# A decoder layer on one core: another task order in the front, other engines for copies, other PSUM banks

## The chip, the cores and the metric

The kernel runs on one core of a Trainium2 chip. The core has five engines, each with its own queue of instructions that it works off in order: PE (TensorE, matrix products; PEld is its weight load), DVE (VectorE), ACT (ScalarE), POOL (GpSimd) and SP (SyncE, which here issues the DMAs). The metric is the device time of one execution in microseconds (us). The kernel before takes 786.61 us, the median of 3 runs (784.54 to 787.06).

## The reference

One layer for 512 positions of width 1024, in float32: an input projection feeds two mixers side by side, an attention with 8 query heads and 2 key/value heads (compressed blocks, selected blocks and a sliding window, each with its own keys and values, mixed by gates), and a diagonal state-space model (S5) with 32 groups of 16 channels and 64 complex states each. Both are normalised, joined and projected; then comes a feed-forward part with a causal convolution of width 3. Cut to what matters:

```
mod = silu(c) @ w_ada + b_ada;  sh1, sc1, gt1, sh2, sc2, gt2 = split(mod, 6)
h = rmsnorm(x, norm1_g) * (1 + sc1) + sh1
zq, zkc, zvc, zks, zvs, zkw, zvw, zg, zs = split(h @ w_in)
o_attn = nsa_attention(zq, zkc, zvc, zks, zvs, zkw, zvw, sigmoid(zg), pe_k, pe_v, w_ck1, w_ck2, w_cv1, w_cv2)
y_ssm = s5_mixer(zs, lam_re, lam_im, log_step, b_re, b_im, c_re, c_im, d_skip, w_glu, b_glu)
x = x + gt1 * (concat(rmsnorm(o_attn), rmsnorm(y_ssm)) @ w_o)
h = rmsnorm(x, norm2_g) * (1 + sc2) + sh2
a, v = split(causal_dwconv(h @ w_up, conv_w, conv_b))
x = x + gt2 * ((silu(a) * v) @ w_down);  return rmsnorm(x, normf_g)
```

In the S5 mixer the state is x(t) = a x(t-1) + B u(t), complex, scanned over the positions; the output is Re(C x) + D u, then GELU and a gated projection (GLU).

## The kernel before

Activations and weights of the large products are split into a high part, rounded to float32r, and a low part, the rest; each product is three float32r matmuls (mm3, L120 to L123: high by high, high by low, low by high). A weight block is loaded by one DMA into a raw buffer, and split into a unit buffer (weights, L111; split, L107): the high half is a cast, whose engine is the entry h_NAME, the low half a subtraction, whose engine is e_NAME. Buffers are few: 4 raw ones, 4 units, 3 small "sw" tiles, and 8 PSUM banks in four groups (acc 3, tr 2, ms 2, pv 1).

The front is written as about 200 small tasks (L143 to L1138), which the string ORDER (L19) calls one after the other (L1140):

- ident to z7: x is normalised and transposed (xn), the modulation columns are computed from w_ada (a and p for the first norm, b and s for the second, g1 for the gate), and z0 to z7 scale one slice of 128 channels each, split it and multiply it for the S5 input (zs, four PSUM banks).
- W, U, L: the block operators of S5 (W0 to W3; We is the copy of a transposed block out of PSUM) and its inputs (U) give the block states X (L).
- zk, zv, kx: keys and values; rope turns q and k (L605), ko is the rotated key, kx transposes it (KS, E), VT holds the values and GT the gates.
- chain (L694): the scan over X. Seven steps l1 to l7 run one after the other, then six short ones (c1 to c6), then eight steps a0 to a7 that add the carried state. Each step is madd (L685): a product (L689), a sum (L691) and an addition to X (L692), on the engine e_l1 to e_a7.
- AM0, AM1 (L727), hid, comp: the compressed blocks plus their position rows, their product with w_ck1 and w_cv1 from raw buffers, a GELU (cg) and a second small product.
- zq, qx: the queries. zq0 to zq3 sum into banks of group acc, of which there are three; rope then reads the bank.
- VV (L957), XV (L964), K, Y: S5's output operators. VV0 to VV7 are two products and a sum each (L348, L349); the second product goes to an "sw" tile (vw). XV copies X in four parts to zu: XV00, XV01, XV10, XV11, each 64 partitions by 1024. K makes the block kernel M through kz and DMAs; Y is the product, yT its transpose, ge the GELU (high and low half yh), gl the GLU (mx is its scaled copy).
- S, O (L807, L872): scores, softmax and output of one query block (qt) and two heads; sm is the scaling of the exponentials, pT the transposed probabilities and pz the compressed ones, copied out of PSUM.
- R, F, N (L1100, L908, L924): the output projection of the S5 half and of the attention half with the addition to x (os, oa), and the second norm (h2).
- eu, eup, cv: the first two up-weight blocks and their products over 384 positions.

After the tasks come two loops over 22 blocks of the feed-forward width: up (L1160; g is the product of the two halves, gc the copy of the gate row) and down (L1203; gh is g split in high and low), and the tail that normalises and stores the output.

Choices stand in the dictionary PICK (L18). kn(name, options) (L30) returns the entry of PICK, or the first option if there is none. e_NAME is the engine of a copy or an elementwise operation (V DVE, A ACT, P POOL), h_NAME the engine of a high half, ps_NAME the group of PSUM banks, r_NAME the kind of buffer.

The order of instructions on each engine is settled when the program is built: the tile layer (schedule_with_timeline_sim, L1304) takes the instructions in the order in which the tasks issue them as priorities, and lets a later one pass where an earlier one is not ready by its own timeline. So instructions of several tasks stand mixed in one queue; on the chip each queue is then strictly in order.

Of the kernel before, what the change touches and what calls it, by code (L numbers as in the profile page):

```python
# [14 lines left out]

PICK = {'ps_mg10': 'pv', 'ps_mg11': 'pv', 'ps_mg13': 'pv', 'ps_mb0': 'pv', 'ps_mb1': 'pv', 'ps_mb2': 'pv', 'ps_mb3': 'pv', 'ps_mc0': 'pv', 'ps_mc1': 'pv', 'ps_mc2': 'pv', 'ps_mc3': 'pv', 'e_bt11a': 'V', 'e_U001': 'A', 'e_U110': 'V', 'e_U111': 'A', 'e_U200': 'V', 'e_U301': 'A', 'e_U310': 'V', 'ps_sc030': 'ms', 'ps_p3101': 'ms', 'e_We5': 'V', 'e_Z0': 'V', 'e_mx1': 'P', 'e_sm10100': 'A', 'ps_hid01': 'tr', 'e_W3': 'V', 'ps_up6': 'ms', 'e_yh1': 'P', 'xn1': 'pt', 'e_inv2': 'P', 'e_g0': 'P', 'ps_p3111': 'ms', 'e_sm00011': 'P', 'e_mx2': 'V', 'e_mx0': 'P', 'e_h21': 'V', 'ps_up7': 'tr', 'e_tl300': 'V', 'e_GT0': 'P', 'e_sm30001': 'V', 'e_ro63': 'P', 'e_ro80': 'P', 'e_ro82': 'P', 'e_ro83': 'P', 'e_XV11': 'V', 'e_Y6': 'V', 'ps_oa3': 'acc', 'e_gh7': 'P', 'e_gh3': 'P', 'e_gh5': 'P', 'e_tl311': 'V', 'e_gt21': 'V', 'e_sm20101': 'P', 'ps_h23': 'tr', 'e_kt1': 'V', 'e_sm21001': 'P', 'ps_p0100': 'ms', 'e_os0': 'V', 'ps_W5': 'tr', 'ps_kx3': 'ms', 'e_GT3': 'P', 'ps_mrp0': 'pv', 'e_tl001': 'V', 'e_tl011': 'V', 'e_tl100': 'V', 'e_tl101': 'V', 'e_tl111': 'V', 'e_tl200': 'V', 'e_inv1': 'P', 'e_inq1': 'P', 'e_inq0': 'P', 'e_inq2': 'P', 'e_inq3': 'P', 'ps_hid10': 'tr', 'e_glu0': 'V', 'e_os3': 'V', 'e_dg0': 'P', 'e_h23': 'V', 'ps_mra1': 'pv', 'ps_eup1': 'pv', 'e_sm21000': 'V', 'e_sm10101': 'V', 'e_XV01': 'P', 'e_Y7': 'V', 'ps_gt21': 'acc', 'e_sm00110': 'V', 'e_kt6': 'V', 'ps_cv': 'ms', 'how_g20': 'VP', 'e_hid01': 'V', 'e_hid11': 'V', 'e_sm30010': 'V', 'tl001': 'sw', 'tl101': 'sw', 'e_sm00111': 'V', 'ps_kx1': 'ms', 'e_E30': 'V', 'e_kt7': 'V', 'ps_ssqa3': 'pv', 'ps_h21': 'tr', 'ps_hid11': 'tr', 'e_kt5': 'V', 'e_dn5': 'P', 'e_h20': 'V', 'ps_h22': 'acc', 'h_ps1010': 'P', 'h_ps2111': 'P', 'h_ink0': 'V', 'h_dn0': 'V', 'e_sm11111': 'P', 'h_h21': 'V', 'h_up20': 'P', 'h_up01': 'V', 'h_up11': 'P', 'h_up30': 'V', 'h_up40': 'V', 'h_up41': 'V', 'h_inq3': 'V', 'e_sm21111': 'P', 'ps_xT2': 'ms', 'ps_xT0': 'ms', 'ps_xT1': 'ms', 'ps_xT3': 'ms', 'e_Z1': 'A', 'e_os20': 'V', 'hx3': 'pt', 'e_E20': 'V', 'e_oT101': 'P', 'h_oa1': 'V', 'h_oa3': 'V', 'ps_pc200': 'pv', 'mixa3': 'pt', 'h_dn2': 'V', 'ps_p2112': 'ms', 'h_gh1': 'V', 'e_dn2': 'P', 'e_os11': 'V', 'h_h20': 'P', 'h_yh2': 'V', 'ps_gt20': 'tr', 'e_Wc0': 'V', 'e_sy2': 'V', 'e_Z3': 'A', 'h_gh0': 'V', 'h_gh4': 'V', 'hx2': 'pt', 'h_dn3': 'P', 'e_g1': 'P', 'e_sm20111': 'P', 'e_sm00000': 'A', 'e_sm00101': 'P', 'e_sm01001': 'P', 'e_sm01011': 'P', 'e_sm01100': 'V', 'e_sm01101': 'P', 'e_sm01110': 'A', 'e_sm10000': 'A', 'e_sm10011': 'P', 'e_sm11000': 'V', 'e_sm11101': 'P', 'e_sm20001': 'P', 'e_sm20011': 'P', 'e_sm21011': 'P', 'e_sm30111': 'P', 'e_sm31111': 'P', 'ps_U0': 'tr', 'e_Y2': 'V', 'e_th101': 'V', 'h_inq0': 'V', 'e_xn0': 'P', 'ps_L2': 'tr', 'e_pt2111': 'P', 'ps_p3102': 'ms', 'e_oT011': 'P', 'e_a7': 'P', 'e_pt1010': 'P', 'e_kt3': 'V', 'e_pt0010': 'P', 'e_kt2': 'V', 'e_inv3': 'P', 'h_yh3': 'V', 'e_XV00': 'P', 'r_adab00': 'mid', 'r_adac00': 'mid', 'r_adac10': 'mid', 'r_adac11': 'mid', 'r_adac21': 'pt', 'r_adac30': 'mid', 'r_adac31': 'mid', 'r_adag100': 'pt', 'r_adag101': 'mid', 'ada_g20': 'V', 'r_adag110': 'mid', 'r_adag111': 'mid', 'ada_g21': 'V', 'r_adag120': 'mid', 'r_adag121': 'mid', 'ada_g22': 'V', 'r_adag130': 'mid', 'r_adag131': 'mid', 'ada_g23': 'V', 'e_up181': 'P', 'r_adab11': 'pt', 'e_l4': 'V', 'h_up180': 'P', 'e_ro60': 'P', 'e_ro81': 'P', 'e_gh2': 'P', 'h_gh15': 'V', 'e_gl2': 'V', 'e_Wc3': 'A', 'e_up111': 'P', 'e_oa2': 'V', 'h_up121': 'V', 'e_Wc1': 'A', 'ps_zv0': 'tr', 'e_up51': 'P', 'e_gh20': 'P', 'h_up140': 'P', 'e_Y1': 'V', 'e_os01': 'V', 'e_U101': 'A', 'e_gh11': 'P', 'ada_c2': 'V', 'ps_pc001': 'ms', 'e_hid00': 'V', 'e_gc3': 'V', 'e_up141': 'P', 'e_Wc7': 'A', 'ps_W2': 'tr', 'h_dn12': 'P', 'e_dn20': 'P', 'e_xn2': 'P', 'h_up141': 'P', 'h_gh8': 'V', 'e_sm31100': 'V', 'h_dn6': 'P', 'h_up81': 'P', 'e_tl310': 'V', 'e_dn10': 'P', 'ps_up9': 'ms', 'e_up190': 'P', 'h_gh10': 'V', 'h_up21': 'V', 'h_up130': 'V', 'h_inv3': 'V', 'h_up101': 'P', 'e_pT2012': 'V', 'h_gh5': 'V', 'e_pz101': 'V', 'e_dn12': 'P', 'e_g8': 'P', 'ps_up4': 'tr', 'e_up21': 'P', 'e_pT3101': 'A', 'ps_up13': 'tr', 'e_up90': 'P', 'h_inv0': 'P', 'e_up50': 'P', 'ps_up8': 'tr', 'e_VV6': 'P', 'e_up60': 'P', 'e_We00': 'V', 'e_up161': 'P', 'h_dn17': 'V', 'ps_up18': 'ms', 'e_sm00001': 'P', 'e_rowa1': 'V', 'js': '0', 'ps_mg20': 'pv', 'e_x2': 'V', 'e_sm10111': 'P', 'e_sm01010': 'V', 'e_W11': 'V', 'e_pz211': 'V', 'h_dn15': 'V', 'e_g13': 'P', 'e_pT3001': 'A', 'e_pT3003': 'A', 'e_sm30110': 'V', 'e_sm20010': 'V', 'e_L11': 'V', 'e_oT3': 'V', 'e_g15': 'P', 'e_os31': 'V', 'e_dg6': 'P', 'e_E10': 'V', 'h_ins0': 'V', 'e_up160': 'P', 'pz100': 'sw', 'ps_L3': 'tr', 'ps_q3': 'ms', 'e_kz2': 'V', 'e_g12': 'P', 'h_up51': 'P', 'h_up190': 'V', 'ps_p1010': 'acc', 'e_We30': 'V', 'e_A4': 'V', 'ps_up19': 'ms', 'ps_pc000': 'ms', 'e_pz300': 'V', 'e_glu1': 'V', 'e_gh4': 'P', 'e_We01': 'V', 'h_inq1': 'V', 'ps_co0': 'ms', 'h_up90': 'V', 'e_We10': 'V', 'e_gt11': 'V', 'e_ko1': 'V', 'e_U211': 'A', 'e_g5': 'P', 'e_up80': 'P', 'e_gl3': 'V', 'e_xn1': 'A', 'e_pT3100': 'V', 'e_a4': 'V', 'h_up31': 'P', 'e_W21': 'V', 'e_mh33': 'V', 'h_gh11': 'V', 'h_up80': 'V', 'e_sm31011': 'P', 'e_up200': 'P', 'e_U010': 'V', 'h_dn1': 'P', 'h_up70': 'V', 'h_ins1': 'P', 'e_kz4': 'V'}  # L18
# [1289 lines left out]
```

## Time and profile before

| | |
|---|---|
| median of 3 runs | 786.61 us |
| profiled execution | 788.21 us, span 786.4 us |
| PE busy | 725.1 us (92%) |
| DVE busy | 473.5 us (60%) |
| ACT busy | 290.2 us (37%) |
| POOL busy | 298.1 us (38%) |
| mean granted clock of PE | 0.957 |
| DMA | 87.64 MB, mean 111 GB/s |

The span is the time from the first to the last instruction. A busy time is the sum of an engine's instructions. PE's ends are modelled, so a busy PE need not run at its peak; the granted clock is a share of full speed. In a timeline row the columns are start and duration in us, engine, line of the kernel, operation, what is written and read, the shape and the count; in brackets stands how long the engine stood idle before it and whose instruction ended that.

### The profile page before, as it was taken

Reading aid. Unit: us, or ns where it says so; the run is one execution under the profiler, and the core shown is the slowest. Engines: PE = TensorE matmul, PEld = TensorE weight load, DVE = VectorE, ACT = ScalarE, POOL = GpSimd, SP = SyncE. Lnnn points to the kernel's source line nnn. Section 1 sums busy time; section 2 is a strip of 40 time slices with the busy share of each in tenths; the row PEclk is TensorE's granted clock in tenths of the full one; section 3 lists DMA queues with packets and bytes.
Section 4 is the critical chain, followed back from the end, with each engine's and each line's share of the span. In section 5 each row is a group of like instructions: output and inputs, shape, how many; then the busy total and the mean of one; then the engine's idle time right before and its main releaser. Section 6 shows DMA issues by size and latency. Waiting matters only on the chain.

```text
span 786.4 us, 11211 instructions
## 1 busy us (share of the span) xinstructions
PE 725.1 (92%) x4155; PEld 566.2 (72%) x4155; DVE 473.5 (60%) x1034; ACT 290.2 (37%) x603; POOL 298.1 (38%) x286
## 2 busy tenths in 40 slices
PE   3897999867899999989979999999999999999993
PEld 2576787555567666757769888888888888888883
DVE  2459938279666878585575576666554454333337
ACT  7443334111576755355423232332242322212123
POOL 2687548887121425254551142120333103130023
PEclk9799999988989999979979999999999999999997
DMA  8665245751121034000053133334232324223102
GB/s 266 234 247 194 95 156 170 288 185 57 29 52 33 1 147 175 2 0 5 1 188 134 54 113 129 138 131 133 108 131 83 108 81 134 108 81 107 54 1 107
DMA packets 30843, 87.64 MB, mean 111 GB/s; under 512 B 4712, under 2 KB 9252, under 8 KB 30757
## 3 DMA queue, kind: packets, MB, share of 16 engines
q1 hardware_dynamic: 30789, 86.92, 32.3%
q8 instruction: 33, 0.54, 0.3%
q14 instruction: 21, 0.17, 0.1%
HBM read 82.71 MB, written 2.10 MB: 108 GB/s over the span
## 4 chain that ended last, share of the span: by engine, by line
PE 75%; DVE 10%; POOL 7%; ACT 3%; DMA 2%; issue 2%; SPq 0%; POOLq 0%; ACTq 0%; DVEq 0%
PE up L123 9%; PE up L121 9%; PE up L122 9%; PE dn L123 5%; PE dn L121 5%; PE dn L122 5%; PE sc L827 3%; PE p L892 2%; PE po L898 2%; DVE vw L348 1%; PE eup L121 1%; PE eup L123 1%; PE eup L122 1%; PE y L1012 1%; POOL prl L689 1%
## 5 line engine op out<-in xcount | busy, mean ns | idle before, releaser
L123 PE MATMUL up<-h2h,uup 128*128 128x512 f32 x320 | 126.4, 395 | 0.0
L121 PE MATMUL up<-h2h,uup 128*128 128x512 f32 x320 | 126.3, 396 | 0.0
L122 PE MATMUL up<-h2l,uup 128*128 128x512 f32 x320 | 126.0, 394 | 0.0
L1175 DVE SCALAR_TENSOR_TENSOR us<-up,cst,us 128x511 f32<-128x511 f32 x80 | 59.8, 747 | 64.4 <-ACT us L1173 63.2
L1173 ACT ACTIVATE us<-up,cst 128x512 f32<-128x512 f32 x40 | 31.1, 778 | 107.9 <-PE up L123 107.9
L123 PEld LDWEIGHTS up<-h2h,uup 128*128 128x128 f32 x320 | 60.1, 188 | 14.1
L122 PEld LDWEIGHTS up<-h2l,uup 128*128 128x128 f32 x320 | 60.0, 188 | 14.2
L121 PEld LDWEIGHTS up<-h2h,uup 128*128 128x128 f32 x320 | 60.1, 188 | 14.0
L123 PE MATMUL dn<-udn,ghs 128*128 128x512 f32 x176 | 68.5, 389 | 0.0
L122 PE MATMUL dn<-udn,ghs 128*128 128x512 f32 x176 | 68.5, 389 | 0.0
L121 PE MATMUL dn<-udn,ghs 128*128 128x512 f32 x176 | 68.0, 389 | 0.0
L109 POOL TENSOR_TENSOR uup<-rup,uup 128x1024 fp32r<-128x1024 f32 x13 | 33.0, 2540 | 49.8 <-ACT uup L64 31.9
L73 POOL TENSOR_SCALAR Ss<-Ss,sm 128x384 f32<-128x384 f32 (+3 forms) x39 | 23.4, 612 | 53.8 <-DVE sm L854 41.3
L827 PE MATMUL sc<-KS,QS 64*128 64x288 f32 (+2 forms) x128 | 38.3, 524 | 1.5 <-DVE mx L843 1.4
L109 DVE TENSOR_TENSOR uup<-rup,uup 128x1024 fp32r<-128x1024 f32 x27 | 32.9, 1219 | 10.8 <-ACT uup L64 9.7
L122 PEld LDWEIGHTS dn<-udn,ghs 128*128 128x128 f32 x176 | 33.0, 188 | 6.9
L123 PEld LDWEIGHTS dn<-udn,ghs 128*128 128x128 f32 x176 | 33.0, 188 | 6.9
L121 PEld LDWEIGHTS dn<-udn,ghs 128*128 128x128 f32 x176 | 33.0, 188 | 6.8
L850 ACT ACTIVATE Ss<-Ss,mx 128x128 f32<-128x128 f32 (+3 forms) x64 | 35.0, 548 | 0.0
L898 PE MATMUL po<-pt,VT 128*64 128x128 f32 x320 | 28.9, 294 | 1.1 <-ACT pt L64 1.1
L71 POOL CAST uup<-rup 128x1024 fp32r<-128x1024 f32 x8 | 9.3, 1163 | 51.1 <-PE up L123 40.7
L898 PEld LDWEIGHTS po<-pt,VT 128*64 128x64 f32 x320 | 19.8, 143 | 11.4 <-issue 4.2
(455 smaller groups left out, 1709.5 us busy)
## 6 DMA issues: line engine op xcount, KB each, us to landing
...
```

The source lines that it names most:

```text
L71: P.tensor_copy(dst, src)
L73: P.tensor_scalar(dst, src, s, 1.0, op0=ALU.mult, op1=ALU.mult)
L109: eng.tensor_tensor(out=lo, in0=src, in1=f(hi), op=ALU.subtract)
L121: PE.matmul(ps, w[0], m[0], start=start, stop=False)
L122: PE.matmul(ps, w[0], m[1], start=False, stop=False)
L123: PE.matmul(ps, w[1], m[0], start=False, stop=stop)
L827: PE.matmul(pss[e][:, :n], v.QS[es, u, qs], v.KS[es, g, c0:c0 + n], start=True, stop=True, tile_position=(e * 64, 0))
L850: A.activation(Sv[:, br, :nk], Sv[:, br, :nk], AF.Exp, bias=mx[:, e, 1 + br:2 + br], scale=0.125, accum_out=sm[:, e, 1 + br:2 + br])
L892: PE.transpose(pc_[:, o:o + 128], v.Ss[:, ui, e, br, kc * 128:(kc + 1) * 128], ident)
L898: PE.matmul(half(e), VT[:, kc, br, g], pT[:, o:o + 128], start=kc == 0 and br == 0, stop=kc == qt > 0 and br == 1)
L1173: A.activation(u_, ps, AF.Identity, bias=cv[:, 3, c_:c_ + 1], scale=cv[:, 2, c_:c_ + 1])
L1175: V.scalar_tensor_tensor(u_[:, d:], ps[:, :S - d], cv[:, 2 - d, c_:c_ + 1], u_[:, d:], op0=ALU.mult, op1=ALU.add)
```

## The change

The functions are the same, line for line. ORDER and 46 entries of PICK differ. The tasks are the same 210; those that moved are z0 (from behind p1 to ahead of it), z2 (ahead of dT), bct1 (behind z7), X and cst (a few places later), wv3 (ahead of g11 and kx1), kx2 (ahead of zv1), AM1 (from behind kx2 and cw to behind AM0), VV (ahead of zv3), yh (ahead of qx1), Y3 (ahead of ys), yT1 (ahead of S10, S11 before O10), gl1 (ahead of gl3) and gl2 (ahead of gl0):

```diff
-ident c x0 xn0 x1 xn1 x3 x2 xn2 xn3 silu rows sp vt p0 a0 ws0 step a1 p1 z0 ws1 z1 dT z2 a2 p2 z3 ws2 bc a3 p3 z4 z5 pw ws3 ri bct0 bct1 z6
-z7 Bb1 Bb2 W W1 W0 wk1 zu A4 U1 cst X U0 W3 KS U2 wk2 mid wk0 wk3 s2 L1 U3 wv0 W2 L2 zk1 L3 L0 g11 kx1 wv3 zk0 kx0 zk3 kx3 wv2 Ss b2 g13 zk2
-VC wv1 zv1 chain kx2 cw AM1 g12 g10 zv0 zv2 zv3 VV VV3 b1 b0 AM0 VV1 hid0 hid1 hid2 hid3 comp wq0 wq3 wq1 wq2 zq0 qx0 zq1 zq3 qx3 zq2 qx2
-VV5 qx1 s3 M VV0 s1 VV6 VV2 b3 K1 s0 XV S00 K2 yh K0 K3 O00 S01 O01 glu0 VV4 S02 glu1 O02 K4 K5 Y1 K6 Y0 S03 O03 VV7 K7 ys Y3 Y2 yT0 S10 yT1
-O10 ge0 yT3 ge1 yT2 S11 S12 ge3 ge2 gl3 O11 S13 xr gl1 gl0 gl2 gt1 wos O12 O13 ssq R1 S20 O20 woa S21 O21 S22 S23 O22 S30 O23 R0 R3 R2 F1
+ident c x0 xn0 x1 xn1 x3 x2 xn2 xn3 silu rows sp vt p0 a0 ws0 step a1 z0 p1 ws1 z1 z2 dT a2 p2 z3 ws2 bc a3 p3 z4 z5 pw ws3 ri bct0 z6 z7
+bct1 Bb1 Bb2 W W1 W0 wk1 zu A4 U1 U0 W3 KS U2 X wk2 mid cst wk0 wk3 s2 L1 U3 wv0 W2 L2 zk1 L3 L0 g11 wv3 kx1 zk0 kx0 zk3 kx3 wv2 Ss b2 g13
+zk2 VC wv1 kx2 zv1 chain cw g12 g10 zv0 zv2 VV zv3 VV3 b1 b0 AM0 AM1 VV1 hid0 hid1 hid2 hid3 comp wq0 wq3 wq1 wq2 zq0 qx0 zq1 zq3 qx3 zq2
+qx2 VV5 yh qx1 s3 M VV0 s1 VV6 VV2 b3 K1 s0 XV S00 K2 K0 K3 O00 S01 O01 glu0 VV4 S02 glu1 O02 K4 K5 Y1 K6 Y0 S03 O03 VV7 K7 Y3 ys Y2 yT0 yT1
+S10 S11 O10 ge0 yT3 ge1 yT2 S12 ge3 ge2 gl1 gl3 O11 S13 xr gl2 gl0 gt1 wos O12 O13 ssq R1 S20 O20 woa S21 O21 S22 S23 O22 S30 O23 R0 R3 R2
```

The entries of PICK, with the default written out where an entry is added or taken away:

```
front, to DVE:   e_KS2 e_QS1 e_VT0 e_We20 e_ko2 e_pT0110 e_pT1010 e_pz301 h_inv1 (from ACT); e_l3 e_l6 e_oa01 e_oa11 e_os2 e_sm21010 (from POOL)
front, to ACT:   e_U110 e_kt7 e_pT3100 (from DVE); e_XV00 e_sm20111 e_sm30111 (from POOL)
front, to POOL:  e_dg2 e_mx2 e_yh3 (from DVE)
front, banks:    ps_K2 ms to tr; ps_p0000 tr to ms; ps_pc110 tr to acc
up and down, to DVE:   h_gh6 h_gh20 h_up170 e_gc1 (from ACT); e_up21 e_up161 h_up11 e_dn10 (from POOL)
up and down, to POOL:  e_gh0 e_gh12 e_gh15 e_g11 e_up201 e_dn18 (from DVE); h_dn8 h_up191 (from ACT)
up and down, to ACT:   h_gh1 (from DVE)
up and down, banks:    ps_up13 tr to acc; ps_up19 ms to acc; ps_up20 acc to tr
```

## Rows read from the trace of the kernel before

**Rows 1.** Busy time by stage: stretch in us, its length, then busy time (and instructions) of PE, PEld, DVE, ACT and POOL, PE's granted clock, the DMA engines' busy share, GB/s.
```profile
0.00:140.00 140.00, 117.70 (x771) 94.35 (x771) 90.20 (x157) 62.15 (x117) 88.28 (x98) 0.95 0.57 194
140.00:200.00 60.00, 45.99 (x284) 31.01 (x282) 37.28 (x50) 9.32 (x17) 46.46 (x53) 0.89 0.46 167
200.00:405.00 205.00, 191.95 (x1427) 135.23 (x1427) 144.19 (x569) 114.31 (x326) 75.59 (x84) 0.93 0.18 55
405.00:640.00 235.00, 235.00 (x1088) 194.92 (x1087) 139.46 (x178) 70.89 (x92) 57.14 (x30) 1.00 0.33 115
640.00:765.00 125.00, 125.00 (x552) 103.19 (x550) 46.94 (x54) 26.14 (x34) 24.08 (x15) 1.00 0.24 81
765.00:787.00 22.00, 9.45 (x42) 7.51 (x40) 15.38 (x28) 7.35 (x18) 6.56 (x7) 0.77 0.25 95
```

**Rows 2.** The list of PE's waits: who waited for whom, total us, times, longest.
```profile
PE xT L458 <- ACT xt L64: 9.5, 1, 9.5
...
PE zq L121 <- DVE rope L613: 5.5, 1, 5.5
PE eup L121 <- ACT eu L64: 4.8, 1, 4.8
...
PE hT L759 <- DVE cg L1244: 3.5, 1, 3.5
```

**Rows 3.** PE's timeline around the fourth group of zq.
```profile
186.42 0.50 PE L394 MATMUL mb<-ones,rowb 128*128 128x1 f32 x4
192.47 0.76 PE L121 MATMUL zq<-uinq,hh 128*128 128x512 f32 x1 [5.55 <-DVE rope L613]
...
196.71 0.39 PE L122 MATMUL zq<-uinq,hh 128*128 128x512 f32 x1
```

**Rows 4.** DVE's timeline: scan step l4 (its product and its addition to X), AM, VV, the copy of X, rope of the first zq, and one vw product later.
```profile
132.39 0.69 DVE L689 TENSOR_TENSOR prl<-A,X 128x512 f32<-128x512 f32 x1 [0.81 <-POOL X L692]
...
133.57 0.43 DVE L692 TENSOR_TENSOR X<-X,adl 128x256 f32<-128x256 f32 x1
...
134.77 4.90 DVE L733 TENSOR_TENSOR mid<-zu,vt 128x992 f32<-128x992 f32 x2 [0.45 <-ACT zu L64]
...
174.54 2.87 DVE L348 TENSOR_TENSOR vw<-RI,C 128x512 f32<-128x512 f32 x1 [5.25 <-POOL X L692]
...
181.00 5.08 DVE L348 TENSOR_TENSOR vw<-RI,C 128x512 f32<-128x512 f32 x2
186.11 2.00 DVE L67 COPY zu<-X 64x1024 f32<-64x1024 f32 x1
...
191.03 0.63 DVE L611 TENSOR_TENSOR rope<-zq,cst 128x512 f32<-128x512 f32 x1
...
191.91 0.41 DVE L613 TENSOR_TENSOR rope<-zq,cst 128x256 f32<-128x256 f32 x1
...
211.07 0.69 DVE L348 TENSOR_TENSOR vw<-RI,C 128x512 f32<-128x512 f32 x1 [1.68 <-DMA M<-kz]
```

**Rows 5.** POOL's timeline: the first and the last instruction of scan step l3, the first of l5, the first and the last of l6, and the two copies of X.
```profile
128.85 1.88 POOL L689 TENSOR_TENSOR prl<-A,X 128x512 f32<-128x512 f32 x1
...
131.62 0.73 POOL L692 TENSOR_TENSOR X<-X,adl 128x256 f32<-128x256 f32 x1
134.14 1.28 POOL L689 TENSOR_TENSOR prl<-A,X 128x512 f32<-128x512 f32 x1 [1.79 <-DVE X L692]
...
140.30 1.27 POOL L689 TENSOR_TENSOR prl<-A,X 128x512 f32<-128x512 f32 x1
...
142.54 0.72 POOL L692 TENSOR_TENSOR X<-X,adl 128x256 f32<-128x256 f32 x1
...
180.48 5.05 POOL L71 COPY zu<-X 64x1024 f32<-64x1024 f32 x2
```

**Rows 6.** ACT's timeline: its part of the copy of X.
```profile
179.04 2.13 ACT L64 ACTIVATE zu<-X 64x1024 f32<-64x1024 f32 x1 [10.87 <-POOL X L692]
```

**Rows 7.** Groups of instructions by line and operation (count; busy us, mean ns of one; idle before, releaser): low halves of up weights on POOL and on DVE, copies of probabilities out of PSUM on ACT and on DVE.
```profile
L109 POOL TENSOR_TENSOR uup<-rup,uup 128x1024 fp32r<-128x1024 f32 x13 | 33.0, 2540 | 49.8 <-ACT uup L64 31.9
...
L109 DVE TENSOR_TENSOR uup<-rup,uup 128x1024 fp32r<-128x1024 f32 x27 | 32.9, 1219 | 10.8 <-ACT uup L64 9.7
...
L64 ACT ACTIVATE pt<-p 128x512 f32<-128x512 f32 x25 | 14.3, 591 | 16.2 <-PE p L892 16.2
...
L67 DVE COPY pt<-p 128x512 f32<-128x512 f32 x15 | 10.3, 683 | 2.5 <-PE p L892 2.5
```

**Rows 8.** PE's timeline: the last matmul of zv and the first of hid.
```profile
139.86 0.29 PE L123 MATMUL zv<-uinv,hl 128*128 128x280 f32 x1
140.08 0.43 PE L747 MATMUL hid<-w_ck,mid 128*64 128x256 f32 x1
```

**Rows 9.** PE's timeline at the first modulation columns.
```profile
29.27 1.01 PE L394 MATMUL ma<-ones,rowa 128*128 128x1 f32 x4 [0.92 <-ACT rowa L64]
31.34 2.24 PE L385 MATMUL ma<-adaa,cs 128*32 128x256 f32 x16 [1.06 <-DVE mod L399]
```

**Rows 10.** The timeline of all engines and queues: the low half of h2, and the first loads of the up weights on SP's queue.
```profile
392.98 1.21 DVE L109 TENSOR_TENSOR h2l<-hx,h2h 128x1024 fp32r<-128x1024 f32 x1
...
394.25 0.83 SPq L115 DMA_DIRECT2D rup<-in_w_up_dram  x2
```

**Rows 11.** Busy time in the stretch 120 to 140 us, columns as in rows 1.
```profile
120.00:140.00 20.00, 19.33 (x158) 15.79 (x155) 18.18 (x20) 8.46 (x21) 17.43 (x13) 1.00 0.50 170
```

More of the change, by code (lines that the diff above doesn't have):

```diff
@@ L24 @@
-O10 ge0 yT3 ge1 yT2 S11 S12 ge3 ge2 gl3 O11 S13 xr gl1 gl0 gl2 gt1 wos O12 O13 ssq R1 S20 O20 woa S21 O21 S22 S23 O22 S30 O23 R0 R3 R2 F1
-S31 O30 F0 O31 S32 S33 O32 O33 cv F2 N0 N1 F3 N2 N3 eu0 eup0 eu1 eup1
+ident c x0 xn0 x1 xn1 x3 x2 xn2 xn3 silu rows sp vt p0 a0 ws0 step a1 z0 p1 ws1 z1 z2 dT a2 p2 z3 ws2 bc a3 p3 z4 z5 pw ws3 ri bct0 z6 z7
+bct1 Bb1 Bb2 W W1 W0 wk1 zu A4 U1 U0 W3 KS U2 X wk2 mid cst wk0 wk3 s2 L1 U3 wv0 W2 L2 zk1 L3 L0 g11 wv3 kx1 zk0 kx0 zk3 kx3 wv2 Ss b2 g13
+zk2 VC wv1 kx2 zv1 chain cw g12 g10 zv0 zv2 VV zv3 VV3 b1 b0 AM0 AM1 VV1 hid0 hid1 hid2 hid3 comp wq0 wq3 wq1 wq2 zq0 qx0 zq1 zq3 qx3 zq2
@@ L26 @@
+qx2 VV5 yh qx1 s3 M VV0 s1 VV6 VV2 b3 K1 s0 XV S00 K2 K0 K3 O00 S01 O01 glu0 VV4 S02 glu1 O02 K4 K5 Y1 K6 Y0 S03 O03 VV7 K7 Y3 ys Y2 yT0 yT1
+S10 S11 O10 ge0 yT3 ge1 yT2 S12 ge3 ge2 gl1 gl3 O11 S13 xr gl2 gl0 gt1 wos O12 O13 ssq R1 S20 O20 woa S21 O21 S22 S23 O22 S30 O23 R0 R3 R2
+F1 S31 O30 F0 O31 S32 S33 O32 O33 cv F2 N0 N1 F3 N2 N3 eu0 eup0 eu1 eup1
 """
```

2 lines of the change are left out of this document (1 added, 1 removed).

## The prediction

> **What bounds the kernel now.** I read the table of stages first [rows 1]: from 405 to 765 us TensorE (PE) is busy in all 360 us, at full clock, with up- and down-projection alone. Nothing that this change does to copies there can shorten it; it can only open a hole. What can move lies before 405: PE idles 22.3 us in 0 to 140, 14.0 of 60 us in 140 to 200, and 13.1 in 200 to 405. The list of PE's waits [rows 2] says what ended the idle time: 9.5 us at the start for the first x tile (not touched), 5.5 us once for VectorE's (DVE) rope of q, 4.8 us for the first up weights, 3.5 us for the compressed hidden's GELU. The largest that the edits touch is the 5.5 us wait.
>
> That wait, in time [rows 3]: zq's fourth group needs a PSUM bank that rope of the first group must free. PE stands from 186.92 to 192.47, and comes back slow: its next matmuls start 0.43 us apart until 196.7, then 0.23. Nine or so pay 0.20 each, 1.8 us. So the place costs up to 5.55 + 1.8 = 7.35 us. The reader should see in DVE's timeline [rows 4] that rope is three short instructions, 191.03 to 192.32, which stand behind DVE's work on VV and the X copy; that DVE began that work only at 174.54, after 5.25 us of waiting for POOL's X at L692 (the scan); and that there it crawls: two vw products take 5.08 us from 181.00, where one costs 0.69 with POOL quiet at 211.07. In those microseconds POOL copies X to zu, two copies in 5.05 us [rows 5].
>
> **The change part by part.** No operation is added or removed; every sum below is a move.
>
> *Two steps of the scan to DVE (e_l3, e_l6) and one copy of X to ACT (e_XV00).* The scan is a serial chain. On POOL step l3 runs from 128.85 to 132.35, 3.50 us, and l6 from 140.30 to 143.26, 2.96 us [rows 5]; l4, on DVE already, runs 132.39 to 134.00, 1.61 us [rows 4]. Two steps at 1.61 save (3.50 - 1.61) + (2.96 - 1.61) = 3.24 us of chain, if DVE takes each at once. What waits at the chain's end is the DVE idle time of 5.25 us at 174.54, so DVE can begin VV up to 3.24 us sooner. XV00 to ACT takes about 2.5 us from POOL, half of 5.05. ACT's own half of that copy took 2.13 us [rows 6], after 10.87 us in which it idled, so ACT hides it. DVE, slowed beside POOL, should get through VV up to 2.5 us sooner. Rope would then start at 191.03 - 3.24 - 2.5 = 185.3 and end near 186.6, just as PE arrives at 186.9: the whole 7.35 us could go. Next late would be the weights of zq, whose low halves POOL computes between scan steps. I take 5.0, two thirds, since DVE's own queue is longer (below), and POOL in that stretch is also held by wq data that does not come earlier. Bounds: 0 (DVE's queue is dealt anew with rope still last) and 7.35. If the scan's early end also hastens the GELU chain of the compressed hidden, which shares DVE with the scan, the 3.5 us wait [rows 2] can go too.
>
> *Copies to DVE.* In the front ACT or POOL hands DVE: We20, KS2, QS1, pT0110, pT1010 (five copies of 128x512 from PSUM at 0.68, against 0.59 on ACT [rows 7]); ko2, VT0, pz301, sm21010 and the high half of inv1 (five smaller ones, taken at 0.4, 2.0 together); oa01 and oa11 (two adds at 0.69, the 512-element product of l4 [rows 4]); the low half of os2 (1.22, from the up weights [rows 7]). That is 3.4 + 2.0 + 1.4 + 1.2 = 8.0 us. DVE hands away U110, kt7, dg2, mx2, yh3 and pT3100, with the last two at 0.68 and the others at 0.2 to 0.5, about 2.8. With l3 and l6 (3.2) DVE has 8.4 us more in 405 us, of which it was busy in 271.7 [rows 1]. Free time covers them wherever DVE is not what PE waits for. Behind each stand the score masks and PSUM copies of the attention, for which PE waits. Bounds: -1 (PE waits less for ACT) and the net 5.2 without the scan steps; I take +1.0, near nothing, because PE idles only 13.1 us after 200 and 4.8 of these are a weight load.
>
> *AM1 behind b1, b0 and AM0.* hid needs both AM products. They end at 139.67 (4.90 us from 134.77 [rows 4]), and PE works on zv up to hid's start at 140.08 [rows 8], so 0.41 us of cover. AM1 last instead of first changes nothing, since both are needed. What can delay them is l3, l6, KS2 and VT0 ahead of them in DVE's queue. Bounds -0.5 and +2.5 (worked out under the third rival); I take +0.5.
>
> Here a rule can be weighed. The trace shows that DVE's add of two SBUF operands takes 0.69 us for 512 elements and 0.43 for 256, so about 1.2 for AM's 992, and that beside POOL's scan it took 2.45 each [rows 4]. The Trainium skill, "SBUF — State Buffer", section "Who interferes with whom", says that a VectorE instruction with two SBUF inputs contends with a GpSimd instruction that reads SBUF, and the later one is held until the first ends. The trace agrees. By this rule l6 on DVE leaves POOL still for that time, AM runs nearer to 1.2 each, and the +2.5 of that rival would be covered; without it the 2.5 stands.
>
> *z0 ahead of p1, z2 ahead of dT, bct1 behind z7.* PE idles 0.92 and 1.06 us at 29 to 31 while it waits for a modulation column [rows 9]; z0 could start earlier, but the stage ends with a3's column and the hh copy. Bounds -2.0 and +1; I take -0.3.
>
> *Task moves without instructions of their own weight* (X, cst, yh, ys, VV; wv3, kx2, Y3, yT1, gl1, gl2). The first five only name a tile, clear one or load constants, long before use; the others swap neighbours that are all needed. 0, within 1 either way.
>
> *oa01, oa11 and the 4.8 us wait.* The first up weights are loaded from 394.25, as soon as h2l of 392.98 frees its buffer [rows 10]; the two adds lie some 30 us before. 0, at best -1.
>
> *From 405 on* (e_up, e_dn, e_gh, h_up, h_dn, h_gh, e_g11, e_gc1, ps_up13, ps_up19, ps_up20). PE has no idle time there; POOL is busy in 57.1 of 235 and 24.1 of 125 us, DVE in 139.5 and 46.9 [rows 1]. A low half that goes from DVE to POOL costs 2.54 against 1.22 [rows 7] and is hidden by that free time. 0; at worst one late operand, +1.3, the difference.
>
> *Sum*: -5.0 + 1.0 + 0.5 - 0.3 = -3.8 us. The profiled execution took 788.21 (span 786.4 and 1.8 around it), so it would take 784.4; it lay 1.6 above the median of 786.61, so the median comes to 782.8.
>
> **The rivals.** *First, more than that*: the scan's early end also frees DVE sooner, and the 3.5 us wait shrinks beside the full 7.35 at zq. 7.35 + 3.5 - 1.5 (the two costs) = 9.3: 777.3. For it: DVE does scan steps and the GELU chain in one queue. Against: the weights for zq are not ready much sooner.
>
> *Second, nothing*: rope still stands behind VV in DVE's queue, since each engine's order is dealt when the program is built and the wait at 186.9 is a place where this order did not fit the chip; or the time is given back in the attention. Then the costs alone remain, less a little: 786.3.
>
> *Third, slower*: DVE becomes the bound of 120 to 140, where it is busy in 18.18 of 20 us [rows 11]. l3 and l6 (3.22), KS2 (0.68) and VT0 (0.41) add 4.31 to 1.82 free, an overhang of 2.5 us. It decides from the point where AM starts more than 0.41 us after 134.77; then hid, the loads of wq behind hid's buffers and zq are all late by the overhang, POOL's scan waits for DVE, and the gain at zq is not had. With half of the 5.2 for the copies lost too: +2.5 + 2.6 - 1 (PE waits less for ACT) = about +4: 790.6. For it: POOL already waited 1.79 us for DVE's l4 [rows 5]. Against: DVE's 18.18 are inflated by POOL at its side.
>
> **How the numbers follow.** Forecast 0.42 (780 to 784.5, centre 782.8), first rival 0.17 (774 to 780), second 0.20 (784.5 to 788.5), third 0.21 (789 to 793). A measurement of this kernel tells about 0.3%, 2.4 us, from no change. Faster by more than that (below 784.25): 0.17 + 0.38 of the forecast's 0.42 + 0.02 = 0.57; slower (above 788.97): 0.21; the same: 0.22. The range for 8 in 10 goes from 774.5 to 790.5; the forecast's own is 780 to 784.5.
>
> **What would show it.** Right: the rope wait of zq under 1 us and no matmuls 0.43 apart behind it; l3 and l6 on DVE near 1.6 us each; one POOL copy of X, not two; DVE's wait for POOL's X gone or under 2 us; 405 to 765 unchanged within 1 us. Wrong: AM ending after 141 with PE idle before hid (third rival); rope still last behind VV (second); new waits of PE on DVE after 200 above 5 us together; or a hole in PE after 405, which I rule out.

## The result and the profile after

The changed kernel takes 779.10 us, median of 4 runs (777.91 to 779.78), against 786.36 for the kernel before, measured beside it: a ratio of 0.991 with a 95% interval of 0.9888 to 0.9931, some 7 us less. The forecast was 782.8 in a range of 774.5 to 790.5. The profiled execution takes 778.83 us with a span of 777.0. Executions of one kernel differ in time, most of them in step with TensorE's mean granted clock, and the ratios leave out the executions that this lengthened most, so that a median and a ratio can disagree.

PE's work can be cut where both kernels do the same thing. In PE's timeline of the changed kernel these are the first matmul of zk, the first of hT, the last of zq, the first transpose of h2 and the first up product:

```profile
80.24 0.50 PE L121 MATMUL zk<-uink,hh 128*128 128x512 f32 x1 [0.71 <-ACT zu L64]
...
164.21 0.47 PE L759 MATMUL hT<-ident,cg 128*128 128x128 f32 x1 [2.82 <-DVE cg L1244]
...
194.84 0.39 PE L123 MATMUL zq<-uinq,hl 128*128 128x512 f32 x1
...
373.81 0.27 PE L939 MATMUL h<-ident,xn 128*128 128x128 f32 x1
...
420.71 0.45 PE L121 MATMUL up<-h2h,uup 128*128 128x512 f32 x1
```

The same five in the kernel before:

```profile
79.48 0.50 PE L121 MATMUL zk<-uink,hh 128*128 128x512 f32 x1 [0.70 <-ACT zu L64]
...
164.26 0.47 PE L759 MATMUL hT<-ident,cg 128*128 128x128 f32 x1 [3.49 <-DVE cg L1244]
...
199.69 0.39 PE L123 MATMUL zq<-uinq,hl 128*128 128x512 f32 x1
...
381.85 0.27 PE L939 MATMUL h<-ident,xn 128*128 128x128 f32 x1
...
430.10 0.45 PE L121 MATMUL up<-h2h,uup 128*128 128x512 f32 x1
```

Differences of these starts (of zq, the end) give the table. The third column is a second profile of the changed kernel, from the experiments.

| stretch, us | before | after | after, second profile |
|---|---|---|---|
| start to zk | 79.48 | 80.24 | 77.99 |
| zk to hT | 84.78 | 83.97 | 84.19 |
| hT to the last zq | 35.82 | 31.02 | 31.22 |
| last zq to h2 | 181.77 | 178.58 | 180.12 |
| h2 to up | 48.25 | 46.90 | 48.14 |
| up to the end | 356.30 | 356.29 | 356.34 |

The largest change is in hT to zq, 4.8 and 4.6 us. Attention (zq to h2) gives 3.2 in one execution and 1.7 in the other, the stretch to hT 0.8 and 0.6. The first row swings by 2.3 us between two executions of one kernel: in the first profile the first zs matmuls, from 35.59 on, start 0.43 us apart, in the second, from 34.53 on, 0.24. The 1.4 us from h2 to up are not there the second time. Neither is credited to the change. Of the kernel before there is one profile.

The stages of [rows 1] read in the changed kernel, in the same columns:

```profile
0.00:140.00 140.00, 116.87 (x767) 93.05 (x767) 93.03 (x161) 60.06 (x112) 82.28 (x96) 0.96 0.57 194
140.00:200.00 60.00, 51.49 (x373) 34.12 (x372) 42.76 (x81) 13.66 (x25) 45.67 (x51) 0.91 0.45 167
200.00:405.00 205.00, 190.83 (x1398) 138.58 (x1398) 146.02 (x560) 113.54 (x323) 70.01 (x79) 0.95 0.21 64
405.00:640.00 235.00, 235.00 (x1072) 193.31 (x1072) 139.01 (x176) 69.80 (x91) 57.27 (x32) 1.00 0.32 110
```

Between 140 and 200 PE is busy for 51.5 us instead of 46.0; the wait for rope is gone. PE's list of waits, which answers to [rows 2], has no rope row at all. It has a new one, for hl on DVE, and a smaller one for cg:

```profile
PE zs L123 <- DVE hl L109: 3.8, 2, 2.9
...
PE hT L759 <- DVE cg L1244: 2.8, 1, 2.8
```

DVE's timeline, against [rows 4]: product and addition of l3, AM, product and addition of l6, the first vw product, and rope:

```profile
130.74 0.68 DVE L689 TENSOR_TENSOR prl<-A,X 128x512 f32<-128x512 f32 x1
...
132.13 0.41 DVE L692 TENSOR_TENSOR X<-X,adl 128x256 f32<-128x256 f32 x1
...
135.45 4.82 DVE L733 TENSOR_TENSOR mid<-zu,vt 128x992 f32<-128x992 f32 x2 [0.45 <-ACT zu L64]
140.84 0.69 DVE L689 TENSOR_TENSOR prl<-A,X 128x512 f32<-128x512 f32 x1 [0.57 <-POOL X L692]
...
142.25 0.41 DVE L692 TENSOR_TENSOR X<-X,adl 128x256 f32<-128x256 f32 x1
...
169.65 2.84 DVE L348 TENSOR_TENSOR vw<-RI,C 128x512 f32<-128x512 f32 x1 [2.87 <-POOL X L692]
...
187.37 0.68 DVE L611 TENSOR_TENSOR rope<-zq,cst 128x512 f32<-128x512 f32 x1
...
188.30 0.41 DVE L613 TENSOR_TENSOR rope<-zq,cst 128x256 f32<-128x256 f32 x1
```

DVE starts VV at 169.65 instead of 174.54 and rope at 187.37 instead of 191.03. Rope ends at 188.71, PE's next zq matmul starts at 188.86, and PE fills the moment before with six modulation products. But the scan has hardly become shorter: the step after l6 starts on POOL at 142.82, 0.5 us sooner than the 143.34 before. What let DVE go was something else. POOL's timeline in the changed kernel (uinq is a low half of zq's weights, X the addition that ends a scan step):

```profile
166.19 2.81 POOL L109 TENSOR_TENSOR uinq<-rinq,uinq 128x1024 fp32r<-128x1024 f32 x1
168.95 0.66 POOL L692 TENSOR_TENSOR X<-X,ada 128x224 f32<-128x224 f32 x1
169.57 2.37 POOL L109 TENSOR_TENSOR uinq<-rinq,uinq 128x1024 fp32r<-128x1024 f32 x1
...
184.70 2.73 POOL L71 COPY zu<-X 64x1024 f32<-64x1024 f32 x1
```

And in the kernel before:

```profile
163.88 2.52 POOL L109 TENSOR_TENSOR uinq<-rinq,uinq 128x1024 fp32r<-128x1024 f32 x1
...
168.69 5.19 POOL L109 TENSOR_TENSOR uinq<-rinq,uinq 128x1024 fp32r<-128x1024 f32 x2
173.84 0.66 POOL L692 TENSOR_TENSOR X<-X,ada 128x224 f32<-128x224 f32 x1
```

The addition to X that DVE waits for stood behind three low halves and now stands behind one. The order of POOL's queue has changed.

### The profile page after: what moved, and what is told of

It reads as the page before. It is cut to its first block, busy times and chain, and to the rows that moved or that the text cites. A ratio compares the mean times of both kernels' runs of the same rounds, so it can differ in the third digit from the quotient of the medians.

```text
span 777.0 us, 11206 instructions
## 1 busy us (share of the span) xinstructions
PE 719.3 (93%) x4155; PEld 562.2 (72%) x4155; DVE 478.3 (62%) x1048; ACT 286.7 (37%) x595; POOL 288.4 (37%) x280
## 4 chain that ended last, share of the span: by engine, by line
PE 74%; DVE 8%; POOL 5%; ACT 4%; issue 3%; DMA 3%; SPq 2%; POOLq 0%; DVEq 0%; ACTq 0%
PE up L123 10%; PE up L121 10%; PE up L122 10%; PE dn L121 5%; PE dn L122 5%; PE dn L123 5%; PE sc L827 2%; PE po L898 2%; SPq L1001 2%; PE p L892 2%; ACT Ss L850 1%; PE eup L121 1%; PE eup L122 1%; PE eup L123 1%; DVE VV L348 1%
## 5 line engine op out<-in xcount | busy, mean ns | idle before, releaser
L109 POOL TENSOR_TENSOR uup<-rup,uup 128x1024 fp32r<-128x1024 f32 x12 | 29.8, 2481 | 48.3 <-ACT uup L64 31.3
L73 POOL TENSOR_SCALAR Ss<-Ss,sm 128x384 f32<-128x384 f32 (+3 forms) x36 | 20.2, 573 | 56.0 <-DVE sm L854 26.0
L109 DVE TENSOR_TENSOR uup<-rup,uup 128x1024 fp32r<-128x1024 f32 x28 | 34.1, 1220 | 7.5 <-ACT uup L64 6.5
L109 DVE TENSOR_TENSOR udn<-rdn,udn 128x1024 fp32r<-128x1024 f32 x17 | 22.8, 1342 | 7.6 <-ACT udn L64 7.4
L892 PE MATMUL p<-ident,Ss 128*128 128x128 f32 x160 | 27.0, 291 | 0.5 <-DVE ots L1088 0.5
```

The source lines that it names most:

```text
L73: P.tensor_scalar(dst, src, s, 1.0, op0=ALU.mult, op1=ALU.mult)
L109: eng.tensor_tensor(out=lo, in0=src, in1=f(hi), op=ALU.subtract)
L892: PE.transpose(pc_[:, o:o + 128], v.Ss[:, ui, e, br, kc * 128:(kc + 1) * 128], ident)
```

## The experiments

Two questions were put. Which part of the change removed the rope wait: the shorter scan and the lighter POOL (theory 1), or POOL's new order (theory 2)? And why do kernels that lose the rope wait not all become faster (theory 3, below)? Most kernels are one of the two kernels with the order, or some of the entries of PICK in which they differ (47, not 46), exchanged. All compute the whole result. The table is worked out from their profiles, one of each, as the stretches above; "VV" is how long after hT's start DVE starts its first vw product, "VV4" how long DVE waits at VV4's product in the first attention block for the DMAs from kz to M, "block" PE's longest wait in that block, "low" the time at PE's lower clock (granted clock 0.50) between 200 and 260 us. The last column is the ratio; the medians of b_l6, b_l6_again and b_seven (785.39, 790.08 and 785.29) are 1.000, 1.006 and 1.000 of the median of the kernel before.

| kernel | hT to zq | VV | rope wait | zq to h2 | VV4 | block | low | time against before |
|---|---|---|---|---|---|---|---|---|
| before | 35.82 | 10.28 | 5.55 | 181.77 | 1.68 | 1.06 | 6.8 | 1 |
| after | 31.02 | 5.44 | 0 | 178.58 | 0.79 | 0.69 | 2.7 | 0.991 |
| after_again | 31.22 | 5.42 | 0 | 180.12 | 0.67 | 0.69 | 7.2 | 0.987 |
| b_scan | 29.33 | 3.70 | 0 | 186.79 | 0.99 | 2.03 | 20.5 | 1.002 |
| b_l6 | 29.95 | 3.70 | 0 | 190.32 | 2.40 | 3.19 | 34.1 | 0.990 |
| b_xv | 34.28 | 10.26 | 3.13 | 183.24 | 0.85 | 1.89 | 13.7 | 1.012 |
| b_order | 30.03 | 5.42 | 0 | 184.02 | 2.23 | 3.00 | 17.1 | 1.005 |
| a_noscan | 35.58 | 10.25 | 4.32 | 181.49 | 1.23 | 1.06 | 3.4 | 1.007 |
| b_pick | 30.45 | 3.69 | 0 | 180.11 | 0.68 | 0.69 | 6.8 | 0.995 |
| b_scanvp | 32.69 | 10.25 | 2.82 | 187.83 | none | 0.69 | 20.5 | 1.011 |
| a_dg2 | 31.34 | 5.42 | 0 | 184.04 | 0.53 | 1.16 | 17.1 | 1.002 |
| b_l6_again | 31.06 | 5.42 | 0 | 188.48 | 2.33 | 3.13 | 30.7 | 0.992 |
| a_qs1 | 29.46 | 3.70 | 0 | 178.33 | 0.20 | 0.69 | 0.4 | 0.996 |
| b_seven | 29.31 | 3.70 | 0.12 | 178.62 | 0.32 | 0.71 | 3.2 | 0.996 |

The columns VV and rope wait fall into two groups by POOL's order. In four profiles (before, b_xv, a_noscan, b_scanvp) the addition to X stands behind three low halves: VV starts 10.25 to 10.28 us after hT, and the rope wait is 2.82 to 5.55. In the other ten it stands behind one: 3.69 to 5.44 us, and no rope wait over 0.12. The step between 3.7 and 5.4 belongs to the execution: the two profiles of b_l6, one program, have one each, and where it is 3.70, hT itself starts later (PE's wait for cg before it is 4.22 us, against 2.82).

**The three entries alone (b_scan).**

```diff
+'e_l3': 'V', 'e_l6': 'V'
-'e_XV00': 'P'
```

> The kernel before with three entries of the change alone: scan steps l3 and l6 to DVE, one copy of X to ACT. Theory 1 (as predicted: the scan chain is 3.24 us shorter and POOL has one copy of 2.5 us less): the stretch from hT's first matmul to zq's last, 35.8 us before, falls to about 31, the whole time by 4 to 5 us. Theory 2 (what counts is POOL's order: the last but one addition to X now stands ahead of two of the four low halves of zq's weights, so that DVE starts VV 4.9 us sooner): the same fall, with that addition near 169 us. Rival (the order of the tasks did it): the rope wait of zq stays above 3 us, time 785 to 787.

Measured: the rope wait gone and the stretch at 29.33 us, as both theories had it, with the addition to X at 166.47. The time did not follow: 785.89 us against 785.64, ratio 1.0018 (0.9993 to 1.0043). In the profile attention took 5.0 us more than before; most of what the three entries won was given back there.

**One scan step alone (b_l6, twice).**

```diff
+'e_l6': 'V'
```

> The kernel before with one entry: scan step l6 to DVE. The chain is then shorter by 1.35 us at most, and POOL keeps both copies of X. Theory 1: the stretch from hT to zq's last matmul gets shorter by 1.4 us, the time by about as much (785). Theory 2: POOL's queue gets the addition to X ahead of two low halves even by this one step, so DVE's VV starts 4 to 5 us sooner and the stretch is shorter by 3 to 5 us, the time 782 to 783.

Measured: one step of 1.35 us takes the whole rope wait away. POOL's timeline shows why, with the addition behind one low half:

```profile
166.50 2.52 POOL L109 TENSOR_TENSOR uinq<-rinq,uinq 128x1024 fp32r<-128x1024 f32 x1
168.99 1.11 POOL L692 TENSOR_TENSOR X<-X,ada 128x224 f32<-128x224 f32 x1
```

Theory 2 holds for the stretch, at 5.9 us (4.8 in the second profile, below). The times fell into two groups, neither at the 782 to 783 of the theory: 776.0 to 778.7 us in three runs, 792.1 to 793.7 in three.

> The kernel before with scan step l6 alone on DVE, once more: its times fell into two groups, 776 to 779 and 792 to 794, and the profile was of the second, with 34 us at the lower clock from 208 us. Theory 3: an execution of the first group has the same queues and the same rope wait (none) and differs by that stretch alone; a profile of it shows less than 10 us at the lower clock between 200 and 250. Rival (the groups differ in waits, DMA arrivals for instance): the stretch is as long and the time is lost elsewhere.

Measured: 777.4 to 793.0 us in 12 runs (median 790.08; ratio 0.992, 0.984 to 0.9995). Its profile (786.3 us) again has a long stretch at the lower clock. Over both runs of this kernel the five executions of 776.0 to 779.1 have a mean granted clock of 0.963 to 0.971, the other thirteen, of 786.3 to 793.7, 0.938 to 0.954. No profile fell on one of the five, so that their queues wait the same is not shown; that the clock goes with the time is.

**One copy alone (b_xv).**

```diff
-'e_XV00': 'P'
```

> The kernel before with one entry: the copy XV00 from POOL to ACT, scan as before, and POOL's addition to X behind the same three low halves as before. Theory 1: DVE gets through VV beside POOL 2.5 us sooner, rope wait 3.0 us, time 784. Theory 2: DVE still starts VV at about 174.5 us; the rope wait falls by less than 1.5 us, time 785 to 786.5.

Measured: VV starts as late as before, and the rope wait falls from 5.55 to 3.13 us. Theory 1 was right on the rope wait (3.0); theory 2 was right on VV and wrong on the rope wait (less than 1.5 off). Both were wrong on the time, which rose to 793.5 us, 1.2% (0.9 to 1.5); PE waits 1.89 us in the first attention block, for ACT, and why the whole lost so much more stays open.

**The order alone (b_order) and the entries alone (b_pick).**

In b_order all of ORDER is the new one and PICK is that of before; the first of the moved tasks:

```diff
-a1 p1 z0 ws1 z1 dT z2
+a1 z0 p1 ws1 z1 z2 dT
...
```

> The kernel before with the new order of the tasks alone, all engines and banks as before. As predicted: the order is worth -0.3 to +0.5 us, time 786 to 787, and the rope wait stays. Rival (the order did most): the stretches from zq's end to the first transposes of h2 and the rope wait shrink, time 780 to 783. In the other kernel POOL's addition to X stands behind one low half with this order too; by theory 2 the rope wait then falls by 2 us or more, time near 784.

Measured: without any of the three entries, both copies of X still on POOL, the rope wait is gone. POOL again:

```profile
170.31 2.79 POOL L109 TENSOR_TENSOR uinq<-rinq,uinq 128x1024 fp32r<-128x1024 f32 x1
173.06 1.59 POOL L689 TENSOR_TENSOR pra<-A,zu 128x448 f32<-128x448 f32 x1
174.61 0.66 POOL L692 TENSOR_TENSOR X<-X,ada 128x224 f32<-128x224 f32 x1
```

With the two groups of the table that settles the first question for theory 2, as far as the start of VV goes; the copy of X to ACT takes its own 2.4 us off the rope wait where the old order stays (b_xv). No run moved the addition alone. The time is 789.62 us, 0.5% more (0.3 to 0.8), and not near 784: PE stands 3.00 us in the first attention block, and zk to hT took 87.9 us. Of that, zk to the first matmul of hid took 65.8 us in this profile, 65.1 in a_dg2 and 64.2 in b_scanvp, 60.4 to 60.6 in the other eleven; PE waits there among others for DMAs of the modulation weights (0.8 to 3.0 us). Whether the edit or the execution makes that is open.

In b_pick PICK is the new one and ORDER that of before, as a diff against the changed kernel:

```diff
-a1 z0 p1 ws1 z1 z2 dT
+a1 p1 z0 ws1 z1 dT z2
...
```

> The changed kernel with the order of the tasks put back. On DVE the scaling of the first softmax block stands ahead of VV4's product as in the changed kernel, on POOL the addition to X stands behind one low half of zq's weights as there. Theories 2 and 3: both gains stay, time 778 to 781. Rival (the order is needed): 783 or more.

Measured: 781.53 us, ratio 0.9953 (0.9931 to 0.9976). The median lies a little above the 781 of the theories, well under the 783 of the rival. The order costs when it stands alone; beside the entries it costs nothing and may add to the gain (779.10 and 779.63 with it, but the intervals of the ratios touch). So the two parts don't add up.

**The change without the three entries (a_noscan).**

```diff
-'e_l3': 'V', 'e_l6': 'V'
+'e_XV00': 'P'
```

> The changed kernel with l3, l6 and XV00 back on POOL. POOL's addition to X then stands behind three low halves, as before; DVE's order in the first softmax block stays as in the changed kernel. Theories 2 and 3: the rope wait is back with 4 to 6 us, the clock in the first attention block stays at its upper level, time 783 to 785. Rival (all of the gain hangs on these three): 786 to 787.

Measured: the rope wait is back with 4.32 us and the stretch with 35.58, and the clock stays up in the first block, all as expected. The time is 791.46, not 783 to 785; ratio 1.0066 (1.0038 to 1.0094). Against the first profile of the changed kernel 4.6 us come from this stretch, 2.9 from attention and 3.0 from before zk, where executions scatter anyway.

**What gives the gain back: the first attention block.** In b_scan DVE reads, in its timeline:

```profile
203.10 0.69 DVE L348 TENSOR_TENSOR vw<-RI,C 128x512 f32<-128x512 f32 x1 [0.99 <-DMA M<-kz]
203.71 0.16 DVE L854 TENSOR_TENSOR sm<-sm,GT 128x6 f32<-128x6 f32 x1
203.82 0.69 DVE L349 TENSOR_TENSOR VV<-VV,vw 128x512 f32<-128x512 f32 x1
204.44 0.22 DVE L855 TENSOR_TENSOR scz<-scz,sm 128x64 f32<-128x64 f32 x1
```

VV4's product needs a buffer that DMAs from kz to M still read; the scaling of the first softmax block is queued behind it, and PE waits for that:

```profile
204.80 0.45 PE L884 MATMUL pc<-ident,scz 128*128 128x128 f32 x1 [2.03 <-DVE scz L855]
```

The clock falls inside this wait, at 203.6. The stretch 210 to 220 us in b_scan, and after it in the changed kernel, where the scaling stands ahead of the product (columns as in [rows 1]; the clock is the third figure from the right):

```profile
210.00:220.00 10.00, 10.00 (x62) 5.99 (x60) 4.44 (x28) 6.48 (x28) 1.86 (x5) 0.50 0.26 48
```

```profile
210.00:220.00 10.00, 9.88 (x136) 6.48 (x133) 7.48 (x57) 7.07 (x31) 2.29 (x6) 1.00 0.27 52
```

PE is busy in both, but at 0.50 it gets through 62 instructions, at 1.00 through 136. In b_l6_again DVE waits longer at the same product, 2.33 us, with the scan of the next scores behind it, and PE stands 3.13 us.

Theory 3 was formed from this: the change pays only if the first attention block is free of such a wait.

**VV4 off DVE (b_scanvp),** on top of b_scan's entries:

```diff
+'e_VV4': 'P'
```

> The kernel before with the three scan and copy entries and one more that the change does not have: VV's fifth group (VV4) on POOL instead of DVE. In the kernel with the three entries alone DVE waits at VV4's first product (0.99 us, for the DMAs that read kz) with the scaling of the first softmax block behind it, PE stands 2.03 us, and its clock is at the lower level for some 20 us. Theory 3 (the rope stall that goes is given back there, as a wait of DVE's queue in the first attention block and the slow clock behind it): without that product in DVE's queue PE waits under 0.8 us there, the slow stretch after 200 us is under 8 us, and the time 779 to 782. Rival (the slow stretch comes whatever waits there): slow stretch as before, time 784 to 787.

A miss for theory 3. The wait for VV4 is gone and PE's longest is 0.69 us, yet the clock stays low for 20.5 us and the time is 794.55, ratio 1.0106 (1.0066 to 1.0146). Three shorter waits (0.47, 0.69 and 0.64) end at 205.03, 206.85 and 207.97, but the clock falls before the second of them (the third figure from the right again):

```profile
204.00:205.00 1.00, 0.56 (x4) 0.11 (x1) 0.88 (x9) 1.00 (x7) 0.00 (x0) 1.00 0.25 49
205.00:206.00 1.00, 0.96 (x3) 0.47 (x3) 0.42 (x3) 1.00 (x6) 0.00 (x0) 0.83 0.30 55
206.00:207.00 1.00, 0.31 (x2) 0.15 (x1) 0.31 (x4) 1.00 (x7) 0.90 (x1) 0.50 0.21 41
```

So here it fell with no wait above 0.47 us in this block ahead of it. This entry also brought the late addition to X back, and 2.82 us of rope wait with it, although the scan entries are all in. So the scan's engines don't decide that; POOL's order does.

**One small task back on DVE (a_dg2).**

```diff
-'e_dg2': 'P'
```

> The changed kernel with one entry put back: dg of the third K group on DVE again. In the changed kernel it runs on POOL at 45.5 us, DVE's product at 45.95 takes 6.29 us beside five POOL instructions in a row (1.13 before), and PE waits 2.92 us for hl behind it. Theory: POOL's dg makes POOL begin first; with dg back on DVE that product takes under 3 us, the wait of 2.92 goes, and zk begins up to 1.3 us sooner: 777.5 to 779. Rival (the long product comes from the order of z0 and p1): as the changed kernel, 779.

Measured: DVE's long product is short again,

```profile
49.04 1.14 DVE L348 TENSOR_TENSOR scv<-RI,Bb 128x512 f32<-128x512 f32 x1
```

and PE's 2.9 us wait for hl is gone, as expected. The rival is out also by b_pick, where the old order stands and the product takes 6.30. But zk began no sooner (80.69), and the time was 787.61 us, ratio 1.0022 (0.9986 to 1.0057). Zk to hid is 4.6 us longer, as said, and in the first attention block PE now waits for DVE, with 17.1 us at the lower clock:

```profile
209.35 0.63 PE L892 MATMUL p<-ident,Ss 128*128 128x128 f32 x4 [1.16 <-DVE dg L985]
```

The profile puts this wait down to dg, which ended last; the transposes do not read dg, and what they need of DVE is more likely the copy out of a PSUM bank ahead of it (208.94 to 209.22), which is queued behind VV4's product. That reading is not tested.

**One copy back on ACT (a_qs1).**

```diff
-'e_QS1': 'V'
```

> The changed kernel with one entry put back: the copy QS1 on ACT. ACT then has four of these copies of 0.58 us among the exponentials of the first block instead of three, and DVE's scan of the next scores stands before VV4's product. Theory 3: PE's wait in the first block grows from 0.69 to over 1 us in one place, a stretch of 7 us or more at the lower clock follows it after 205 us, time 782 to 786; the rope wait stays gone. Rival (the block does not hang on one copy): 778 to 781.

Measured: 782.94 us, in the expected range, but not for the expected reason. PE's wait stays at 0.69, the clock between 200 and 250 stays up, attention takes 178.33 us as in the changed kernel. What differs lies before hT (zk starts at 82.81, zk to hT takes 85.59). The block does not hang on this copy. In a later block PE waits 1.73 us, up to 225.78, for a scaling on DVE, and the clock does not fall behind that (1.00 from 220 to 240).

**Seven entries (b_seven).**

```diff
-'e_XV00': 'P'
+'e_l3': 'V', 'e_l6': 'V', 'e_KS2': 'V', 'e_QS1': 'V', 'e_VT0': 'V', 'e_dg2': 'P'
```

> The kernel before with seven entries of the change: l3, l6, XV00, and the copies KS2, QS1, VT0 and dg2. Against the kernel with the first three this puts VV4's product on DVE behind the scaling of the first softmax block. Theory 3: rope wait none, PE's longest wait in the first block under 1.5 us, lower clock after 200 us under 10 us, time 779 to 782. Rival (the other entries or the order are needed): a wait of 2 us or more there, time 784 to 787.

Measured: the profile (780.7 us) is as theory 3 has it: a rope wait of 0.12 us, no wait over 0.71 us in the block, both stretches as short as in the changed kernel. But only four of 12 executions were at 776.8 to 780.7; four took 785 to 787, four 791 to 795. The ratio is 0.9957 (0.9917 to 0.9997).

**The changed kernel again (after_again).**

> The changed kernel once more, unchanged, to see what one execution of it is worth. Theory 3 (the second half of the gain is the clock in the first attention block): the trace again shows no stretch at the lower clock between 200 and 250 us, and the time is 778 to 781. Rival (that was luck of one execution): such a stretch appears, time above 783.

Measured: 779.63 us, 777.22 to 781.42 in six runs, ratio 0.987 (0.981 to 0.993; by the medians, against 785.57, 0.992). The time is as expected, the clock not quite: there is no low stretch from 200 up to 222 us, but one of 6.8 us then, behind a wait of 1.08 us for the DMAs to M. What sets this kernel apart is that all ten of its runs lie within 4.2 us; next comes b_pick, with ten within 5.5. The kernel before, in 29 runs, took 782.3 to 788.9 us in 21 and 794.6 to 797.4 in eight.

Taken together: PE's longest wait in the first block was 1.9 to 3.2 us in five profiles, and in all five the clock fell inside that wait, for 10.2 to 34.1 us. With 0.7 us or so as the longest it did not fall before 222 us in five profiles, and for 20.5 us in b_scanvp; of three with 1.06 to 1.16 us it fell in two within 3 us (6.8 and 17.1 us). Against it stand b_scanvp and the 1.73 us of a_qs1. That a long wait in this block brings the clock down is thus likely, that it alone decides is not so, and what decides how long the clock stays down is open. The sum of the two stretches from hT to h2 is 208 to 211 us where both the rope wait and the long low stretch are missing (after twice, b_pick, a_qs1, b_seven), and 214 to 221 everywhere else. No version tried beats the changed kernel in all its executions.

## Why the prediction was right and where it was not

The sign and the place were right, the size was short: 3.8 us forecast, some 7 measured. The term that carried the forecast came out at its value in part by luck, and a second gain, in attention, was forecast as a cost.

- *The rope wait, -5.0.* Measured -4.8 and -4.6. The value held, the step behind it only in part. The 3.24 us of chain were to come "if DVE takes each at once": DVE didn't. X was ready for l3 at 129.52 and DVE, behind VV and five small instructions, took it at 130.74; with a copy dealt in between, each step ran 1.8 us, not 1.61. The scan won 0.5 us by the clock time of its next step, 1.2 against the start of hid. The rest of the 4.9 us by which DVE starts VV sooner is POOL's order, which the prediction had read only as "wq data that does not come earlier". b_l6 and b_order, with one entry and with none of the three, show that an edit which changes this order does it; the agreement of 5.0 with 4.8 is partly luck.
- *One copy of X to ACT.* Half of POOL's 5.05 us was priced, 2.5; b_xv shows 2.4 of the rope wait gone by this entry. In the changed kernel no rope wait is left for it to shorten.
- *DVE's wait for POOL's X.* Forecast gone or under 2 us. It is still 2.87, only 4.9 us earlier.
- *The weights of zq next late.* So it is: PE waits 0.41 us for POOL's uinq at 169.05.
- *Copies to DVE, +1.0.* This step failed: attention became shorter, by 3.2 and 1.7 us. As the term had it, PE stood idle there for longer, 8.1 and 9.5 us instead of 6.9. But PE was busy for 4.4 and 4.3 us less with the same products, at a higher mean granted clock. From the last zq to h2, before, after, and after in the second profile (columns as in [rows 1]):

```profile
200.07:381.85 181.78, 174.86 (x1351) 121.35 (x1351) 125.71 (x539) 104.25 (x306) 63.60 (x74) 0.94 0.16 48
```

```profile
195.23:373.81 178.58, 170.47 (x1341) 119.82 (x1342) 123.35 (x543) 104.55 (x307) 59.42 (x70) 0.96 0.17 49
```

```profile
193.40:373.52 180.12, 170.59 (x1340) 120.07 (x1341) 123.79 (x544) 104.57 (x306) 59.42 (x70) 0.96 0.16 49
```

  The sum counted engine time and left out the clock. Where DVE's queue stands in the first block is part of what decides how long PE waits, and PE can run at half speed for up to 34 us from such a wait on (b_l6). The last of [rows 4] held the wait: DVE's product at 211.07 carries 1.68 us for the DMAs from kz to M. It was read for its duration alone. That the copies and not the rest of the change raised the clock is not shown.
- *AM1, +0.5.* AM ends at 140.27 and PE goes from zv to hid at 140.73 without a gap; from zk to hid the kernels take 60.60 and 60.49 us. So nothing, and with it the third rival falls.
- *The rule on the shared port.* The Trainium skill, "SBUF — State Buffer", section "Who interferes with whom", was taken to say that l6 on DVE leaves POOL still and AM runs nearer 1.2 us each. AM took 4.82 us for two, against 4.90 before: l6 came behind AM, and POOL had l5 beside it, from 134.76 to 140.81. The trace does not speak against the rule; its use here was wrong.
- *The first rival, GELU.* Not shown. PE's wait for cg is 2.82 and 2.83 us in the two profiles of the changed kernel, against 3.49, but the two profiles of b_l6, one program, have 4.22 and 2.82.
- *z0 and z2, -0.3.* Not seen; the start of zk scatters by 2.3 us between executions. A new wait of 2.92 us for hl stands there, and it comes from an entry, not from the order: dg2 on POOL, which the prediction counted as 0.2 to 0.5 us that DVE hands away (see the last section).
- *405 to 765 unchanged.* Right: 356.30 and 356.29 us from the first up product. The twenty entries of that stage together cost and gain nothing, with PE busy in all 235 us from 405 to 640.
